# Every third feed-forward weight unit: the remainder by an accumulating on-chip transfer in place of a VectorE subtraction

## The chip, the core and the metric

The kernel runs on one core of one Trainium2 chip. The metric is the device time of one execution in microseconds (us). Before the change two timed runs took 1229.28 and 1230.01 us; their median is 1229.64 us.

## The reference

One layer of a decoder, on 256 tokens of width 2048, all in float32. The input is normalised and multiplied by one wide projection; three groups of heads (RWKV-7, gated DeltaNet, differential attention) work on the result; an output projection and a SwiGLU feed-forward follow, each added to the residual stream:

```
h = rms_norm(x, attn_norm_w)
p = h @ w_in
mixed = concatenate([rwkv7(p_rw), gated_deltanet(p_gdn), differential_attention(p_diff)])
x = x + mixed @ w_out
h = rms_norm(x, ffn_norm_w)
gate, up = split(h @ w_ffn_in)            # 2048 x 11264
x = x + (silu(gate) * up) @ w_ffn_out     # 5632 x 2048
```

The feed-forward reads w_ffn_in and w_ffn_out once, 138 MB of the 217 MB of all loads.

## The kernel before, in words

**Products in three parts.** A float32 number is held as a rounded part (`hi`, type float32r) and a remainder (`lo`). Activations and weights are both split so, and a product is the sum of three TensorE passes: hi by hi, lo of the weights by hi of the activations, hi of the weights by lo of the activations.

**Units.** The weights come as 410 units. A unit is two blocks of 128 rows by 512 columns: a tile of 128 partitions by 1024 float32, 512 KB. TensorE spends 12 matmuls of 512 columns on one: two halves of the tokens, two blocks, three passes, in the order hi, lo, hi for each block. Units 146 to 409 belong to the feed-forward: 176 of w_ffn_in and 88 of w_ffn_out.

**The weight stream.** `fetch_upto` (L218) issues the load of a unit into a buffer `raw` on SyncE's queue (L231). `stage_upto` (L234) splits a unit: ScalarE copies `raw` to `hi`, which rounds it (L245), and VectorE writes `lo` = `raw` - `hi` (L246). `take` (L250) is called when the products of unit u are written out, and stages unit u+3 (`LA` = 3). There are four buffers for `hi` and four for `lo`, so `hi` and `lo` of unit u+3 go where those of unit u-1 were, and can be written only when TensorE has read these for the last time. From unit 150 on (`plan["far"]` = 146 + `LA` + 1) loads run five units further ahead (`FAR` = 8), in nine buffers `raw`: the load of unit u+9 goes where unit u was, and waits until unit u has been split.

**Around it.** In the feed-forward ScalarE also has the SiLU (L121) and the rounding of the hidden columns (L1252), VectorE the products with the gate (L1267), the remainders of the hidden columns (L1253) and the residual sums (L1273). GpSimd's queue (POOL) holds only a few fills early in the program, and none in the feed-forward. What each engine runs, in which order, follows from the order of the calls and a scheduler that places the side work; each engine then runs its list in order, and an instruction waits on semaphores of the engines and transfers that it needs.

Of the kernel before, what the change touches and what calls it, by code (L numbers as in the profile page):

```python
# [8 lines left out]
F32 = mybir.dt.float32  # L9
F32R = mybir.dt.float32r  # L10
AF = mybir.ActivationFunctionType
ALU = mybir.AluOpType
# [81 lines left out]


class Acts:
    """Activation calls grouped by the table set that they need."""

    def __init__(self, tc):
        self.tc, self.nc = tc, tc.nc  # L100
# [27 lines left out]
def trunk(tc, A, out, dbg=None):  # L128
    nc = tc.nc
    V, S, G, TE = nc.vector, nc.scalar, nc.gpsimd, nc.tensor  # L130
# [38 lines left out]
        tog[0] ^= 1  # L169
        return rwbank() if tog[0] else gdbank()  # L170

    # ------------------------------------------------------------------ constants
    cst = pc.tile([P, CONST.shape[1]], F32, name="cst")
    vec = pc.tile([P, NV], F32, name="vec")

# [22 lines left out]
    rs1, lnr1, rsq64, ss2, rs2 = rst[:, 0:2], rst[:, 2:4], rst[:, 4:6], rst[:, 6:8], rst[:, 8:10]  # L198
    ssq = pc.tile([P, 8], F32, name="ssq")

    # ------------------------------------------------------------------ weight stream
    cm_raw, p_raw = pool("raw", 4)
    cm_hi, p_hi = pool("hi", 4)
    cm_lo, p_lo = pool("lo", 4)
# [2 lines left out]
    units = []  # L207
# [7 lines left out]
    state = {"fetched": 0, "next": 0}  # L215
# [19 lines left out]
    def stage_upto(i):  # L235
        fetch_upto(min(i + FIRST - LA, 2 * len(START) - 1))
        fetch_upto(i + FAR - LA if i >= plan["far"] else i)
        while state["next"] <= min(i, len(units) - 1):
            u = state["next"]
            srcs, nk, ns = units[u]  # L240
            n = sum(ns)
            hi = p_hi.tile([P, 1024], F32R, tag="hi", name=nm("hi"))
            lo = p_lo.tile([P, 1024], F32R, tag="lo", name=nm("lo"))
            r, h, l = raws.pop(u), hi[:, :nk * n], lo[:, :nk * n]
            S.copy(h, r)  # L245
            V.tensor_tensor(l, r, h.bitcast(F32), op=ALU.subtract)  # L246
            staged[u] = (h.rearrange("p (k c) -> p k c", c=n), l.rearrange("p (k c) -> p k c", c=n))
            state["next"] += 1

# [31 lines left out]
        plan["ffn"].append((h0, nh, ins_, outs_))  # L281
        h0 += nh

    # ------------------------------------------------------------------ side work, emitted between weight units
    jobs = []

    def spawn(gen, steps=0):
# [21 lines left out]
            advance(g)  # L309

    def after(first, then):
        """Keep the order of two instructions of one engine."""
        first, then = getattr(first, "ins", first), getattr(then, "ins", then)
        act._dep(then, first)

    def products(banks, ul, i, xs, n=512, parts=False):
        """What unit i of a chunk adds to its banks."""
        u, k0, nk = ul[i]
        wh, wl = take(u)
        if parts:  # L320
            seq = [(t, k, p_) for k in range(nk) for p_ in range(3) for t in range(2)]
        else:
            seq = [(t, k, p_) for t in range(2) for k in range(nk) for p_ in (0, 2, 1)]
        seen = [0, 0]
        for t, k, p_ in seq:
            seen[t] += 1
            xh, xl = xs(k0 + k)
            state["mm"] = TE.matmul(banks[t][:, 0:n], lhsT=(xl if p_ == 1 else xh)[:, t * P:(t + 1) * P],  # L328
                                    rhs=(wl if p_ == 2 else wh)[:, k, :], start=(i == 0 and seen[t] == 1),
                                    stop=(i == len(ul) - 1 and seen[t] == 3 * nk))  # L330

    def proj(ul, xs):
        """One chunk of 512 columns in token layout: two banks."""
        banks = [mmbank(), mmbank()]
        for i in range(len(ul)):
            products(banks, ul, i, xs)
            tick()
        return banks

    def rsq(out_, in_, scale=1.0, bias=None, b2=None):  # L340
        """out = (in*scale + bias)^-1/2 [* exp(b2)]"""
        act(out_, in_, AF.Ln, scale=scale, bias=eps_c[:in_.shape[0]] if bias is None else bias)
        if b2 is None:
            act(out_, out_, AF.Exp, scale=-0.5)
        else:
            act(out_, out_, AF.Exp, scale=-0.5, bias=b2)

    # ------------------------------------------------------------------ start: x and its norm
    cm_hT, p_hT = pool("hT")
    hTh = p_hT.tile([P, KT, T], F32R, name="hTh")  # L350
    hTl = p_hT.tile([P, KT, T], F32R, name="hTl")
# [6 lines left out]
    cm_x, p_x = pool("xp", side="right")  # L358
    x_in = A["x"].rearrange("(t p) d -> t p d", p=P)
    xT_in = A["xT"].rearrange("(k p) t -> p k t", p=P)  # L360
    # the array's clock rises while the first loads are on their way
    V.memset(xs1, 0.0)
    b = rwbank()
    for _ in range(WARM):
# [1 line left out]
    nc.scalar.dma_start(vec, A["vecs"])  # L366
    act.window(SET_NLE)
    def load_x():
        """x, transposed, in step with the units of the first chunks; then the constants."""
        xTs = {}  # L370

        def fetch_x(q):
            if q < len(START):
                k0, n = START[q]
                xTs[q] = p_x.tile([P, 2, T], F32, tag="xT", name=nm("xT"), bufs=FIRST // 2 + 1)
                (nc.sync if q else nc.scalar).dma_start(xTs[q][:, 0:n, :], xT_in[:, k0:k0 + n, :])
                fetch_upto(2 * q + 1)

        for q in range(FIRST // 2):
            fetch_x(q)  # L380
        for q, (k0, n) in enumerate(START):
            fetch_x(q + FIRST // 2)
            xT = xTs.pop(q)
            xsq = p_x.tile([P, 2, T], F32, tag="xsq", name=nm("xsq"), bufs=2)
            for j in range(n):
                k = k0 + j
                S.activation(hTh[:, k, :], xT[:, j, :], AF.Copy, scale=vcol("attn_w", k))
                V.scalar_tensor_tensor(hTl[:, k, :], xT[:, j, :], vcol("attn_w", k), hTh[:, k, :].bitcast(F32),
                                       op0=ALU.mult, op1=ALU.subtract)
            act(xsq[:, 0:n, :], xT[:, 0:n, :], AF.Square)  # L390
            for j in range(n):
                V.tensor_tensor(xs1, xs1, xsq[:, j, :], op=ALU.add)
            if q < 2:
                stage_upto(2 * q + 1)
            if q:
                yield
        nc.sync.dma_start(cst, A["const"])
        yield
        nc.sync.dma_start(lora[0:64, :], A["w_lora_b"])
        nc.sync.dma_start(lora[64:128, :], A["a_lora_b"])  # L400
        nc.sync.dma_start(glora, A["g_lora_b"])

    def first_norm():
# [7 lines left out]
        V.tensor_scalar(rsq64, rsq64, 1.0 / 64.0, None, op0=ALU.mult)  # L411
        V.tensor_scalar(lnr1, lnr1, -0.5, None, op0=ALU.mult)
        yield
        # small derived vectors
        V.tensor_scalar(omu, vcol("mu", 0, 14), -1.0, 1.0, op0=ALU.mult, op1=ALU.add)
        V.tensor_scalar(oka, vcol("k_a", 0, 4), -1.0, 1.0, op0=ALU.mult, op1=ALU.add)
        V.tensor_scalar(qw8, vcol("qn"), 0.125, None, op0=ALU.mult)
# [22 lines left out]
        products(banks_lora, plan["lora"], i, hx, 264, parts=True)  # L440
    close(cm_x)

    # ------------------------------------------------------------------ RWKV
    cm_tok, p_tok = pool("tok")
    cm_rq, prq = pool("rwq")
    sgx = prq.tile([P, T], F32, name="sgx")
# [38 lines left out]
    G.memset(XT[96:128, :, 0:32], 0.0)  # L485

    def tokens(banks, n=512):
        """Normalised rows of a chunk, one tile per 128 tokens."""
        res = []
        for t in range(2):  # L490
            tk = p_tok.tile([P, 512], F32, tag="tok", name=nm("tok"), bufs=TOKB)
            S.activation(tk[:, 0:n], banks[t][:, 0:n], AF.Copy, scale=rs1[:, t:t + 1])
            res.append(tk)
        return res

    def turned(toks, i, bank):
        """Column tiles 2i, 2i+1 of a chunk, columns on the partitions: bank[:, j*256 + t]."""
        for j in range(2):
            for t in range(2):
                TE.transpose(bank[:, j * T + t * P:j * T + (t + 1) * P],  # L500
                             toks[t][:, (2 * i + j) * P:(2 * i + j + 1) * P], ident)
        return bank
# [9 lines left out]

    KKRv = KKR.rearrange("p a c s t -> p (a c) s t")

    # inverse of the unit triangular blocks of 32, all at once, by forward substitution
    def forward_sub(n, fill, drain, Fa, Fx, Ft, per):
        scr = tc.dram_tile([n, 32, 32], F32, name=nm("scr"))
        scr2 = tc.dram_tile([n, 32, 32], F32, name=nm("scr2"))
# [142 lines left out]
    def rw_recur():  # L661
# [20 lines left out]
            return 2 * hp + par  # L682

        def read(c, which, rows):
            """Chunk c's tokens on the rows given: state times (r or kk), plus the part within the chunk."""
            b = rwbank()
            for hp in range(4):
                if c > 0:
                    TE.matmul(b[rows, hp * P:(hp + 1) * P], lhsT=KKR[:, hp, c, which, :], rhs=Sbd[:, hp, :],  # L689
                              start=(hp == 0), stop=False, skip_group_check=True)  # L690
            for h in range(8):
                TE.matmul(b[rows, h * 64:(h + 1) * 64], lhsT=AH[:, c, h % 2, h // 2, 64 * which:64 * which + 64],  # L692
                          rhs=VU[:, c, h, :], start=(c == 0 and h == 0), stop=True, skip_group_check=True)
            return b[rows, :]
# [56 lines left out]
    ready["rr"] = tokens(proj(plan["rr"], hx))  # L751
    ready["rv"] = tokens(proj(plan["rv"], hx))

    # ------------------------------------------------------------------ gated delta net
    banks_z = proj(plan["gz"], hx)
    while "rw_v" not in ready:
        tick()
# [281 lines left out]
            S.activation(mh, bv, AF.Copy, scale=vcol("gn"))  # L1039
            V.scalar_tensor_tensor(ml, bv, vcol("gn"), mh.bitcast(F32), op0=ALU.mult, op1=ALU.subtract)  # L1040

    # ------------------------------------------------------------------ differential attention
    def diff_evac(j, banks, res):
        qns = []
        for t in range(2):
# [138 lines left out]
            dj = spawn(diff_evac(j, banks, res), 1)  # L1184
        ready["d", g] = ops

    # ------------------------------------------------------------------ output projection
    def mixs(k):
        if k < 8:
            return mixh_a[:, k, :], mixl_a[:, k, :]  # L1190
# [46 lines left out]
    for cm in (cm_d, cm_mixrg, cm_rq, cm_tok):  # L1237
        close(cm)

    # ------------------------------------------------------------------ feed forward  # L1240
    cm_f, pf = pool("ffn")
    act.window(SET_SILU)
    out_v = out.rearrange("(t p) d -> t p d", p=P)
# [84 lines left out]
```

## Time and profile before

| | |
|---|---|
| timed runs | 1229.28 and 1230.01 us |
| profiled execution, first to last instruction (span) | 1227.3 us |
| timed median less this span | 2.3 us |
| TensorE busy | 1221.7 us, 100% of the span |
| VectorE busy | 710.2 us, 58% |
| ScalarE busy | 589.8 us, 48% |
| GpSimd busy | 5.8 us |
| mean granted clock of TensorE | 0.999 of full speed |
| data moved | 222.4 MB, 181 GB/s over the span |

The page is read from the chain that ended last: it says on which engine the end of the program hangs. Busy time of a matmul is modelled and overlaps with the next one (390 ns each, though a new one starts every 227 ns), so how close TensorE is to its limit is read from the starts of its matmuls, not from its busy share. The profiled execution has no time of its own beside the span; the 2.3 us between it and the median of the timed runs is taken for what lies around it.

### The profile page before, as it was taken

How to read it: one execution, taken by the hardware profiler on the slowest of the kernel's cores; microseconds unless marked ns; L12 is line 12 of the kernel's file. 1: busy time of each engine (PE TensorE's matmuls, PEld its weight loads, DVE VectorE, ACT ScalarE, POOL GpSimd, SP SyncE). 2: the span in 40 equal slices, each digit the busy share in tenths (PEclk: the TensorE clock that was granted, in tenths of full speed). 3: DMA queues.
4: the chain of work that ended last, by engine and by line, in shares of the span. 5: the costliest groups of instructions: out<-in, count | busy, mean ns of one | idle time of the engine just before them, and what ended most of it. 6: DMA issues, size and time to landing. Idle time of an engine off the chain costs nothing.

```text
span 1227.3 us, 15743 instructions
## 1 busy us (share of the span) xinstructions
PE 1221.7 (100%) x6062; PEld 1006.7 (82%) x6062; DVE 710.2 (58%) x972; ACT 589.8 (48%) x799; POOL 5.8 (0%) x11
## 2 busy tenths in 40 slices
PE   9999999999999999999999999999999999999998
PEld 8887888788888878888888888888888888888887
DVE  8585965699565766554454454544445445545553
ACT  7764454665446556544444444433344444444332
POOL 0100000000000000000000000000000000000000
PEclk9999999999999999999999999999999999999999
DMA  9755564256555545766666666566666666665660
GB/s 323 211 150 157 167 196 118 72 152 187 174 162 188 164 129 172 280 199 189 186 190 190 189 188 191 188 194 196 193 190 189 191 188 188 195 190 185 212 195 34
DMA packets 125082, 222.41 MB, mean 181 GB/s; under 512 B 15664, under 2 KB 19888, under 8 KB 125008
## 3 DMA queue, kind: packets, MB, share of 16 engines
q1 hardware_dynamic: 116848, 217.15, 58.6%
q10 hardware_dynamic: 8160, 4.27, 1.2%
q8 instruction: 47, 0.77, 0.2%
q14 instruction: 27, 0.22, 0.1%
HBM read 218.50 MB, written 2.88 MB: 180 GB/s over the span
## 4 chain that ended last, share of the span: by engine, by line
PE 99%; DMA 1%; ACT 0%; DVE 0%; issue 0%; SPq 0%
PE mm L328 90%; PE rw L500 1%; PE gd L500 1%; PE rw L692 1%; PE rw L622 1%; PE rw L1085 1%; PE rw L689 0%; PE rw L705 0%; DMA xT<-in_xT 0%; PE rw L562 0%; DMA vec<-in_vecs 0%; PE rw L1120 0%; PE gd L1120 0%; PE rw L676 0%; PE rw L668 0%; ACT s L121 0%
## 5 line engine op out<-in xcount | busy, mean ns | idle before, releaser
L246 DVE TENSOR_TENSOR lo<-raw,hi 128x1024 fp32r<-128x1024 f32 (+2 forms) x410 | 493.9, 1208 | 432.8 <-ACT hi L245 429.0
L245 ACT CAST hi<-raw 128x1024 fp32r<-128x1024 f32 (+2 forms) x410 | 425.2, 1039 | 535.3 <-PE mm L328 509.7
L328 PE MATMUL mm<-hi,hTh 128*128 128x512 f32 (+1 forms) x1152 | 448.9, 394 | 0.2
L328 PE MATMUL mm<-hi,hTl 128*128 128x512 f32 (+1 forms) x1152 | 441.4, 388 | 0.0
L328 PE MATMUL mm<-lo,hTh 128*128 128x512 f32 (+1 forms) x1152 | 441.1, 387 | 0.0
L328 PEld LDWEIGHTS mm<-hi,hTh 128*128 128x128 f32 x1152 | 215.6, 188 | 44.6 <-issue 1.1
L328 PEld LDWEIGHTS mm<-hi,hTl 128*128 128x128 f32 x1152 | 215.2, 188 | 45.1 <-issue 0.6
L328 PEld LDWEIGHTS mm<-lo,hTh 128*128 128x128 f32 x1152 | 215.4, 188 | 42.8 <-issue 1.1
L328 PE MATMUL mm<-hi,hidh 128*128 128x512 f32 x352 | 137.3, 390 | 0.0
L328 PE MATMUL mm<-hi,hidl 128*128 128x512 f32 x352 | 137.0, 389 | 0.0
L328 PE MATMUL mm<-lo,hidh 128*128 128x512 f32 x352 | 137.0, 389 | 0.0
L328 PEld LDWEIGHTS mm<-hi,hidl 128*128 128x128 f32 x352 | 66.1, 188 | 13.9
L328 PEld LDWEIGHTS mm<-hi,hidh 128*128 128x128 f32 x352 | 66.1, 188 | 13.6
L328 PEld LDWEIGHTS mm<-lo,hidh 128*128 128x128 f32 x352 | 66.1, 188 | 13.5
L328 PE MATMUL mm<-hi,mixh_a 128*128 128x512 f32 x64 | 26.0, 406 | 0.0
L328 PE MATMUL mm<-hi,mixh_d 128*128 128x512 f32 x64 | 25.9, 408 | 0.0
L328 PE MATMUL mm<-hi,mixl_d 128*128 128x512 f32 x64 | 25.4, 400 | 0.0
L328 PE MATMUL mm<-lo,mixh_d 128*128 128x512 f32 x64 | 25.4, 396 | 0.0
L328 PE MATMUL mm<-hi,mixl_a 128*128 128x512 f32 x64 | 25.3, 395 | 0.0
L328 PE MATMUL mm<-lo,mixh_a 128*128 128x512 f32 x64 | 25.2, 394 | 0.0
L121 ACT ACTIVATE sg<-mm,rst 128x512 f32<-128x512 f32 x22 | 15.2, 691 | 10.7 <-PE mm L328 10.7
L778 DVE SCALAR_TENSOR_TENSOR cacc<-gd,vec,cacc 128x255 f32<-128x255 f32 (+2 forms) x36 | 16.2, 477 | 5.8 <-ACT cacc L776 5.5
(301 smaller groups left out, 729.4 us busy)
## 6 DMA issues: line engine op xcount, KB each, us to landing
raw<-in_w_ffn_in SPq DMA_DIRECT2D x176, 512.0 KB, 3.8
raw<-in_w_in SPq DMA_DIRECT2D x103, 512.0 KB, 3.7
raw<-in_w_ffn_out SPq DMA_DIRECT2D x88, 512.0 KB, 4.5
raw<-in_w_out SPq DMA_DIRECT2D x32, 512.0 KB, 4.0
raw<-in_w_in SPq DMA_DIRECT2D x9, 256.0 KB, 5.7
xr<-in_x SPq DMA_DIRECT2D x8, 256.0 KB, 5.1
out<-xr ACTq DMA_DIRECT2D x8, 256.0 KB, 3.7
xT<-in_xT SPq DMA_DIRECT2D x7, 256.0 KB, 5.6
```

Of the source, the lines that this page charges most:

```text
L121: r = self.nc.scalar.activation(out, in_, func, **kw)
L245: S.copy(h, r)
L246: V.tensor_tensor(l, r, h.bitcast(F32), op=ALU.subtract)
L328: state["mm"] = TE.matmul(banks[t][:, 0:n], lhsT=(xl if p_ == 1 else xh)[:, t * P:(t + 1) * P], rhs=(wl if p_ == 2 else wh)[:, k, :], star ...
L500: TE.transpose(bank[:, j * T + t * P:j * T + (t + 1) * P], toks[t][:, (2 * i + j) * P:(2 * i + j + 1) * P], ident)
L622: TE.matmul(b[:, hp * P:(hp + 1) * P], lhsT=KB[rows, hp, c, :, :].rearrange("p s t -> p (s t)"), rhs=KKR[rows, hp, c, :, :].rearrange("p s ...
L692: TE.matmul(b[rows, h * 64:(h + 1) * 64], lhsT=AH[:, c, h % 2, h // 2, 64 * which:64 * which + 64], rhs=VU[:, c, h, :], start=(c == 0 and ...
L778: V.scalar_tensor_tensor(acc[:, sft:T], src[:, 0:T - sft], vcol("conv", 4 * ct + 3 - sft), acc[:, sft:T], op0=ALU.mult, op1=ALU.add)
L1085: TE.matmul(bk[m][:, hx_ * W:(hx_ + 1) * W], lhsT=qT[r, h, i * P:(i + 1) * P], rhs=kT_[r, h, 0:W], start=True, stop=True)
```

## The change

For units 150, 153, ..., 408 (87 of the 264 feed-forward units) VectorE no longer writes `lo`. ScalarE writes the negated, rounded weights into `lo`, and a transfer issued on GpSimd's queue then adds `raw` to `lo` in place, from on-chip memory to on-chip memory. The other units keep the subtraction. Comments that the diff also drops are left out here.

```diff
             S.copy(h, r)
-            V.tensor_tensor(l, r, h.bitcast(F32), op=ALU.subtract)
+            if u >= plan["far"] and u % 3 == 0:
+                S.activation(l, r, AF.Copy, scale=-1.0)
+                G.dma_start(l, r, accum_op=ALU.add)
+            else:
+                V.tensor_tensor(l, r, h.bitcast(F32), op=ALU.subtract)
             staged[u] = (h.rearrange("p (k c) -> p k c", c=n), l.rearrange("p (k c) -> p k c", c=n))
```

VectorE's list has 87 subtractions fewer (323 for 410), ScalarE's 87 instructions more, POOL's 87 transfers more. The lines behind the edit are four higher in the changed kernel (L332 is L328 before).

ScalarE, in the second half of the feed-forward (loads of w_ffn_out). The number in a name is a buffer's; `raw_6997` of before and `raw_7039` of the change hold the same unit. Before:

```order
L245 CAST hi_7035<-raw_6943 128x1024 [waits DMAHW5_49,DVE_49,PE_49]
L245 CAST hi_7053<-raw_6961 128x1024 [waits DMAHW6_49,DVE_49,PE_49]
L245 CAST hi_7071<-raw_6979 128x1024 [waits DMAHW7_49,DVE_49,PE_49]
L245 CAST hi_7089<-raw_6997 128x1024 [waits DMAHW0_49,DVE_49,PE_49]
L245 CAST hi_7107<-raw_7015 128x1024 [waits DMAHW1_49,DVE_49,PE_49]
L245 CAST hi_7129<-raw_7033 128x1024 [waits DMAHW2_49,DVE_49,PE_49]
L245 CAST hi_7147<-raw_7051 128x1024 [waits DMAHW3_49,DVE_49,PE_49]
```

The same place in the changed kernel:

```order
L247 ACTIVATE lo_7078<-raw_6984 128x1024 [waits DMASW6_49,DMAHW5_49,DVE_49,PE_49]
L245 CAST hi_7077<-raw_6984 128x1024 [waits PE_49,Activation_49]
L245 CAST hi_7096<-raw_7002 128x1024 [waits DMAHW6_49,PE_49,Activation_49]
L245 CAST hi_7114<-raw_7020 128x1024 [waits DMAHW7_49,DVE_49,PE_49]
L247 ACTIVATE lo_7133<-raw_7039 128x1024 [waits DMASW7_49,DMAHW0_49,DVE_49,PE_49]
L245 CAST hi_7132<-raw_7039 128x1024 [waits PE_49,Activation_49]
L245 CAST hi_7151<-raw_7057 128x1024 [waits DMAHW1_49,PE_49,Activation_49]
L245 CAST hi_7173<-raw_7075 128x1024 [waits DMAHW2_49,DVE_49,PE_49]
L247 ACTIVATE lo_7192<-raw_7094 128x1024 [waits DMASW0_49,DMAHW3_49,DVE_49,PE_49]
```

The negated copy of such a unit (L247) stands ahead of the rounding of the same unit (L245), not behind it.

SyncE's queue, at the loads that go where those units were (names with DMAHW are semaphores of loads, DMASW those of the transfers on POOL's queue). Before:

```order
L231 DMA raw_6979<-in_w_ffn_out 128x2x512 [waits DMAHW7_49,DVE_49]
L231 DMA raw_6997<-in_w_ffn_out 128x2x512 [waits DMAHW0_49,DVE_49]
L231 DMA raw_7015<-in_w_ffn_out 128x2x512 [waits DMAHW1_49,DVE_49]
L231 DMA raw_7033<-in_w_ffn_out 128x2x512 [waits DMAHW2_49,DVE_49]
L231 DMA raw_7051<-in_w_ffn_out 128x2x512 [waits DMAHW3_49,DVE_49]
```

The same loads in the changed kernel:

```order
L231 DMA raw_7020<-in_w_ffn_out 128x2x512 [waits DMAHW7_49,DVE_49]
L231 DMA raw_7039<-in_w_ffn_out 128x2x512 [waits DMAHW0_49,DMASW0_49,Activation_49]
L231 DMA raw_7057<-in_w_ffn_out 128x2x512 [waits DMAHW1_49,DVE_49]
L231 DMA raw_7075<-in_w_ffn_out 128x2x512 [waits DMAHW2_49,DVE_49]
L231 DMA raw_7094<-in_w_ffn_out 128x2x512 [waits DMAHW3_49,DMASW1_49,Activation_49]
```

Every third load now waits for the end of an accumulating transfer (DMASW), nine units back, and the two loads behind it in the queue wait with it.

TensorE, at the first matmuls of such a unit in the changed kernel:

```order
L332 MATMUL mm_7170<-hi_7114,hidl_4564 128x512
L332 MATMUL mm_7169<-hi_7132,hidh_4563 128x512 [waits Activation_49]
L332 MATMUL mm_7169<-lo_7133,hidh_4563 128x512 [waits DMASW3_49]
L332 MATMUL mm_7169<-hi_7132,hidl_4564 128x512
L332 MATMUL mm_7169<-hi_7132,hidh_4563 128x512
L332 MATMUL mm_7169<-lo_7133,hidh_4563 128x512
```

The second matmul of the unit waits for the transfer where it waited for VectorE; the order of the matmuls is that of before.

## Rows read from the trace of the kernel before

**Rows 1.** The page: span, busy engines, then the chain by line.

```profile
span 1227.3 us, 15743 instructions
PE 1221.7 (100%) x6062; PEld 1006.7 (82%) x6062; DVE 710.2 (58%) x972; ACT 589.8 (48%) x799; POOL 5.8 (0%) x11
...
PE mm L328 90%; PE rw L500 1%; PE gd L500 1%; PE rw L692 1%; PE rw L622 1%; PE rw L1085 1%; PE rw L689 0%; PE rw L705 0%; DMA xT<-in_xT 0%; PE rw L562 0%; DMA vec<-in_vecs 0%; PE rw L1120 0%; PE gd L1120 0%; PE rw L676 0%; PE rw L668 0%; ACT s L121 0%
```

**Rows 2.** Engines' busy time by stretch; behind POOL: clock, DMA share, GB/s.

```profile
550.00:1200.00 650.00, 650.00 (x2907) 538.10 (x2906) 321.19 (x289) 271.16 (x276) 0.00 (x0) 1.00 0.64 191
```

**Rows 3.** Timeline of TensorE over a change of unit; start, duration, engine, line.

```profile
799.07 0.39 PE L328 MATMUL mm<-lo,hidh 128*128 128x512 f32 x1
799.29 0.39 PE L328 MATMUL mm<-hi,hidl 128*128 128x512 f32 x1
799.52 0.39 PE L328 MATMUL mm<-hi,hidh 128*128 128x512 f32 x1
799.75 0.39 PE L328 MATMUL mm<-lo,hidh 128*128 128x512 f32 x1
...
807.91 0.39 PE L328 MATMUL mm<-lo,hidh 128*128 128x512 f32 x1
```

**Rows 4.** Timeline of ScalarE and VectorE there; brackets: idle before, and what ended it.

```profile
799.72 1.05 ACT L245 CAST hi<-raw 128x1024 fp32r<-128x1024 f32 x1 [1.67 <-PE mm L328]
800.81 1.22 DVE L246 TENSOR_TENSOR lo<-raw,hi 128x1024 fp32r<-128x1024 f32 x1 [1.49 <-ACT hi L245]
802.44 1.05 ACT L245 CAST hi<-raw 128x1024 fp32r<-128x1024 f32 x1 [1.67 <-PE mm L328]
```

**Rows 5.** Groups of instructions, 550 to 1200 us; busy, mean ns, idle before.

```profile
L246 DVE TENSOR_TENSOR lo<-raw,hi 128x1024 fp32r<-128x1024 f32 x235 | 288.0, 1225 | 327.5 <-ACT hi L245 324.4 <-DMA out<-xr 3.1
L245 ACT CAST hi<-raw 128x1024 fp32r<-128x1024 f32 x236 | 248.7, 1054 | 370.6 <-PE mm L328 370.6
```

**Rows 6.** Line 387 alone: a scaling copy on ScalarE, min, median, max ns.

```profile
L387 ACT ACTIVATE hTh<-xT,vec x16: 492/500/509, 5.3 to 28.8; 128x256 fp32r<-128x256 f32 x16
```

**Rows 7.** Transfers, 550 to 1200 us: the queue's share, then the loads' landing.

```profile
q1 hardware_dynamic: 63376, 122.17, 63.0%
...
DMA to landing us min/median/max: 3.5/3.9/5.9
```

**Rows 8.** Transfers, 500 to 517 us: rate, the queue's share, the loads' landing.

```profile
DMA packets 3422, 6.61 MB, mean 389 GB/s; under 512 B 205, under 2 KB 205, under 8 KB 3420
q1 hardware_dynamic: 3420, 6.59, 104.3%
...
DMA to landing us min/median/max: 5.1/10.0/10.9
```

**Rows 9.** Issues of loads on SyncE's queue, 550 to 1200 us, in ns.

```profile
L231 SPq DMA_DIRECT2D raw<-in_w_ffn_in x144: 367/368/368, 552.5 to 1080.2; - x144
```

**Rows 10.** Waits of SyncE's queue, 550 to 1200 us: total, times, longest.

```profile
SPq L231 <- DVE lo L246: 537.3, 232, 2.9
```

**Rows 11.** Groups of instructions on POOL, whole span.

```profile
L810 POOL MEMSET XG<- 128x1024 f32 x1 | 1.0, 957 | 156.8 <-DVE sm L848 156.8
```

## The prediction

> **What bounds the kernel now.** I read the chain that ended last first: it lies on TensorE almost from end to end, 90% of it in the unit products of L328 [rows 1]. Next the feed-forward by itself, where the whole change lies: from 550 to 1200 us TensorE is busy throughout at a granted clock of 1.00, while VectorE is busy 321 of 650 us, ScalarE 271, and the 16 transfer engines 0.64 of the time [rows 2]. The timeline shows matmul after matmul 0.23 us apart, across the border between two units too [rows 3]; a unit takes 2.72 us, the distance of two roundings [rows 4]. No gap is there that faster staging could close. The groups say the same: VectorE's subtraction sits idle for ScalarE's rounding, and the rounding for TensorE [rows 5]. Staging is driven by TensorE, which gives buffers back. So a gain has nowhere to come from. What is open is whether the longer way to `lo` still ends before TensorE needs it.
>
> **The slack of a unit before.** TensorE's last reading of a `lo` buffer starts at 799.07, of the `hi` buffer at 799.29 [rows 3]; the rounding into that `hi` starts at 799.72, 0.43 us after [rows 4]. The subtraction ends at 800.81 + 1.22 = 802.03. The unit is taken up three units later: its first `lo` matmul starts at 807.91 [rows 3], 799.75 plus three times 2.72. The present way has 5.9 us to spare.
>
> **What goes.** 87 subtractions of 1.225 us, 107 us of VectorE's time [rows 5]. They lie beside TensorE's work with 5.9 us to spare, so they are worth 0. Where VectorE's wait goes is of no matter, since nothing late hangs on it.
>
> **What comes on ScalarE.** 87 negated copies of 128x1024. The nearest rows are the rounding of the same shape, 1.05 us [rows 5], and a scaling copy of a quarter of it, 0.50 us [rows 6], whose four pieces would be 2.0; I take 1.05, since one instruction pays its start once. In a period of three units (8.16 us) ScalarE goes from 3.2 to 4.2 us for weights, and the rounding that is now behind the copy ends 1.05 us later, with over 6 us to spare. That costs 0; the cover is the three units of staging ahead.
>
> **The path of the transfer.** It starts when its `lo` buffer is free: 799.07 + 0.43 = 799.50 by the lag of the rounding. The copy ends at 800.55. TensorE needs the sum at 807.91. So from the end of the copy to landing the transfer has **7.36 us** at no cost. Call its real time D. If D is longer, TensorE stands still at the unit's second matmul, with all products behind it. Such a stop s puts off the need of the next accumulated unit, but not its start: its buffer is that of the unit before the stopped one, already read. So two stops in a row add up to D - 7.36, the mean stop is **(D - 7.36) / 2**, and 87 of them cost 43.5 us for each us of D above 7.36.
>
> **What D is.** No row shows a transfer on POOL's queue or an accumulation; I build D from the loads. With the transfer engines full, from 500 to 517 us, 389 GB/s pass [rows 8]: 512 KB (524 thousand bytes) take 1.35 us. The fastest landing of a load is 3.5 us [rows 7], so 2.15 us of it is not data. SyncE's issue is 0.37 us [rows 9]; for POOL's I take 0.96, its one instruction on a tile of this shape [rows 11], between the 0.37 of SyncE and, for two sources to describe, twice 0.96; it adds 0.6: 2.75 us beside the data. The data: an accumulation reads `raw` and also the `lo` that it adds to, so twice a load, 2.70 us. That makes 5.45 us alone. The bounds: below, one load's data and least landing, 3.5 us; above, a landing at full engines, 10.9 us [rows 8].
>
> The row for a load prices one source, and an addition that read its target for nothing would cost 1.35 and be hidden; a second source costs the stop. By the Trainium skill (Collectives: The Full Stack, Part 3, the bandwidth ceiling) an adding transfer runs at about half the rate of a copy, because of its two source reads and not of the addition; no run here shows that, and it would leave the sum as it is.
>
> **Sharing.** Loads come three to a period, 4.05 us of full engines, so with the transfer 6.75 of 8.16 us are taken: the engines can carry it. When they carry it matters. A load now waits for the landing of the transfer whose `raw` it overwrites, and two more queue behind it; before, SyncE waited for each subtraction apart, at most 2.9 us [rows 10]. So three loads bunch at each landing, and with D near 8 that is when the next transfer starts. If the two queues share the engines evenly, the 2.70 us become 5.40, and D = 2.75 + 5.40 = 8.15 us. I take this end rather than 5.45, as the bunching makes it. The held loads themselves are hidden: the slot is next read six units, 16.3 us, after the unit's own need, against a landing of at most 10.9.
>
> **The sum.** (8.15 - 7.36) / 2 = 0.40 us of stop, times 87: 34 us. Removed work 0, ScalarE 0, loads 0. 1227.3 + 34 = 1261.3 us of span, and 2.3 around it: **1264 us**, 2.8% over the median of 1229.64. The 2.3 is that median less the span of the one profiled execution.
>
> **Rivals.** (a) *The transfer is hidden.* At D up to 7.36 the time stays at about 1230; up to 7.93 it is less than 2% above (24.6 us are 0.283 us on each of 87). For it: 5.45 us if the loads don't collide, and also 5.45 if the accumulation costs the engines one load's data and does share. Against it: the bunching, and that every part of POOL's way is unmeasured. What decides is whether loads are in flight between copy and landing. By the Trainium skill (DMA: Bandwidth & Descriptors, Anatomy of one DMA) a transfer from GpSimd takes about 2.0 us and its bytes at 436 GB/s, an estimate of 3.2 us for one such tile; the trace's least load, 3.5 us, agrees, and by that rule even two sources shared evenly, some 6.8 us, stay hidden.
>
> (b) *The accumulation is slow in the transfer engines.* If it costs four loads' data instead of two, 5.40 us, a period needs 4.05 + 5.40 = 9.45 us of the engines, 1.29 us over 8.16, and 87 periods cost 112 us at least: 1342. By the path, 2.75 + 5.40 + 4.05 = 12.2 us give 2.42 us a stop, 210 us: 1440. It decides from an engine time above 4.1 us. For it: no row shows the rate of an addition. Against it: nothing in the trace asks for it.
>
> (c) *Faster by over 2%.* It would need 25 us from TensorE, which has no gaps in the feed-forward, at full clock. Only a shorter time between matmuls could give it, and the change does not touch them.
>
> **Chances.** Forecast (a stop of 0.28 to about 1.2 us, 1254 to 1335): 0.42. Hidden, or nearly: 0.40. Slow engines: 0.17. Faster: 0.01. So within 2% (about what a measurement of this kernel tells from no change) 0.40, slower 0.59. The range runs from 1228, just under no change, to 1345, where the slow case begins, which leaves out 0.18; the forecast's own range is 1254 to 1335.
>
> **What would show it.** The changed profile should show POOL's queue with 87 issues and a landing near 8 us; above 7.4 there must be idle time on TensorE before the `lo` matmul of every third feed-forward unit, released by that transfer, about 0.4 us each, and none before the other units. VectorE's busy time should fall by 107 us, ScalarE's rise by 91. SyncE's queue should wait on the transfer once in three loads, with three issues close together behind it. The share of the transfer engines should rise from 0.64 to about 0.8; well above that and near 1, rival (b) holds. The prediction is wrong if landing stays under 7 us, if TensorE waits for something else, such as a rounding or a load, or if the units before 150 change.

## The result, and the profile after

The changed kernel takes 1298.08 us (1296.03 to 1300.13, two runs) against 1229.64: 1.0556 times the time of before, with a 95% interval of 1.0516 to 1.0596. That is 68 us more. The forecast was slower, 1264 us, and the range 1228 to 1345 holds the result; of the loss, 34 us were forecast, half of what came.

The page of the changed kernel: span, busy engines, then the chain that ended last by engine and by line. It answers to [rows 1].

```profile
span 1298.3 us, 15999 instructions
PE 1242.3 (96%) x6062; PEld 1009.3 (78%) x6062; DVE 605.0 (47%) x885; ACT 670.9 (52%) x886; POOL 80.8 (6%) x98
...
issue 50%; PE 41%; POOL 5%; DMA 2%; ACT 1%; DVE 0%; POOLq 0%; SPq 0%; ACTq 0%
PE mm L332 34%; POOL lo L248 5%; DMA lo<-raw 1%; DMA raw<-in_w_ffn_in 1%; PE rw L696 1%; PE rw L626 1%; PE rw L1089 0%; PE rw L693 0%; PE rw L369 0%; PE rw L709 0%; PE rw L504 0%; PE rw L566 0%; POOLq L248 0%; ACT hi L245 0%; PE gd L504 0%
```

The span grew by 71.0 us. TensorE was not busy for 5.6 us of it before (1227.3 less 1221.7) and for 56.0 now: 50.4 us of the growth are standstill, 20.6 are busy time (longer matmuls, and at each stop the end of a matmul that no longer overlaps with the next). VectorE lost 105 us of work, and nothing came of that. The chain, which was TensorE's product line for 90%, now runs over POOL's transfer too; half of it is put to "issue", time for which the profile names no cause, so the reading below goes by TensorE's waits.

The waits of the changed kernel from 500 us on (engine and line, what was waited for, total us, times, longest), and the transfer's own rows (issue time in ns, then issue to landing):

```profile
PEld mm L332 <- DMA lo<-raw: 67.7, 42, 6.1
PE mm L332 <- DMA lo<-raw: 50.3, 36, 5.7
```

```profile
L248 POOL DMA_DIRECT2D lo<-raw x87: 859/859/1002, 502.6 to 1281.9; - x87
...
DMA to landing us min/median/max: 4.5/7.6/10.6
```

The 50.3 us of standstill all wait for the accumulating transfer, at 36 places of 87, 1.4 us each in the mean. And the landing is no one number: 4.5 to 10.6 us.

One such stop in the timeline, ScalarE, POOL and TensorE (brackets: idle before, and what ended it):

```profile
898.88 1.06 ACT L247 ACTIVATE lo<-raw 128x1024 fp32r<-128x1024 f32 x1 [1.44 <-PE mm L332]
```

```profile
900.24 0.86 POOL L248 DMA_DIRECT2D lo<-raw  x1 [7.30 <-ACT lo L247]
908.81 0.86 POOL L248 DMA_DIRECT2D lo<-raw  x1 [7.71 <-ACT lo L247]
```

```profile
907.26 0.39 PE L332 MATMUL mm<-hi,hidl 128*128 128x512 f32 x1
907.48 0.39 PE L332 MATMUL mm<-hi,hidh 128*128 128x512 f32 x1
909.81 0.50 PE L332 MATMUL mm<-lo,hidh 128*128 128x512 f32 x1 [1.94 <-DMA lo<-raw]
```

The negated copy ends at 899.94, POOL issues 0.3 us later, and TensorE goes on at 909.81, when the sum has landed 9.5 us after the issue. The next transfer is issued at 908.81, before that. It lands in 5.7 us and stops nobody.

SyncE's queue and the transfer queues (megabytes, share of 16 engines) from 550 to 1265 us, which answer to [rows 10] and [rows 7]:

```profile
SPq L231 <- DMA lo<-raw: 541.0, 79, 10.8
SPq L231 <- DVE lo L250: 39.0, 25, 3.2
```

```profile
q1 hardware_dynamic: 64431, 124.20, 53.7%
q0 software_dynamic: 11376, 41.42, 31.1%
```

SyncE waits for the landings, once for each transfer (78 are issued there), and hardly for VectorE any more. A transfer takes 0.311 x 715 / 78 = 2.85 us of all engines.

**What a landing depends on.** I took from the trace, for the 82 transfers between the first two and the last three, how many loads were issued just before the transfer, which here and below means from 2.0 us before its own issue to 0.3 us after it, and the mean landing:

| loads issued just before | transfers | mean landing, us |
|---|---|---|
| 0 | 16 | 5.9 |
| 1 | 32 | 7.0 |
| 2 | 11 | 9.1 |
| 3 | 23 | 8.7 |

At the very end, with no load in flight, it is 4.5 us. The loads that the transfer before has held come out when it lands; if the next one is issued within two microseconds after, it runs among them. The row of two is really one of three: all eleven have a third load between 2.4 us before and 0.8 us after their issue. Counted from 2.0 us before to 1.2 us after, none, one, two and three loads stand beside 7, 26, 8 and 41 transfers, which land in 5.9, 6.3, 7.6 and 8.7 us.

### The profile page after: what moved, and what is told of

It reads as the page before. It is cut to its first block, busy times and chain, and to the rows that moved or that the text cites. A ratio compares the mean times of both kernels' runs of the same rounds, so it can differ in the third digit from the quotient of the medians.

```text
span 1298.3 us, 15999 instructions
## 1 busy us (share of the span) xinstructions
PE 1242.3 (96%) x6062; PEld 1009.3 (78%) x6062; DVE 605.0 (47%) x885; ACT 670.9 (52%) x886; POOL 80.8 (6%) x98
## 4 chain that ended last, share of the span: by engine, by line
issue 50%; PE 41%; POOL 5%; DMA 2%; ACT 1%; DVE 0%; POOLq 0%; SPq 0%; ACTq 0%
PE mm L332 34%; POOL lo L248 5%; DMA lo<-raw 1%; DMA raw<-in_w_ffn_in 1%; PE rw L696 1%; PE rw L626 1%; PE rw L1089 0%; PE rw L693 0%; PE rw L369 0%; PE rw L709 0%; PE rw L504 0%; PE rw L566 0%; POOLq L248 0%; ACT hi L245 0%; PE gd L504 0%
## 5 line engine op out<-in xcount | busy, mean ns | idle before, releaser
L250 DVE TENSOR_TENSOR lo<-raw,hi 128x1024 fp32r<-128x1024 f32 (+1 forms) x323 | 387.0, 1203 | 574.0 <-ACT hi L245 568.5
L245 ACT CAST hi<-raw 128x1024 fp32r<-128x1024 f32 (+2 forms) x410 | 422.6, 1033 | 410.4 <-PE mm L332 249.9
L332 PE MATMUL mm<-lo,hTh 128*128 128x512 f32 (+1 forms) x1152 | 447.0, 393 | 35.7 <-DMA lo<-raw 35.6
L332 PE MATMUL mm<-hi,hTh 128*128 128x512 f32 (+1 forms) x1152 | 451.1, 396 | 0.0
L332 PE MATMUL mm<-hi,hTl 128*128 128x512 f32 (+1 forms) x1152 | 444.0, 390 | 0.0
L332 PEld LDWEIGHTS mm<-lo,hTh 128*128 128x128 f32 x1152 | 216.5, 189 | 90.6 <-DMA lo<-raw 47.9
L332 PEld LDWEIGHTS mm<-hi,hTh 128*128 128x128 f32 x1152 | 216.9, 189 | 45.4 <-issue 1.1
L332 PEld LDWEIGHTS mm<-hi,hTl 128*128 128x128 f32 x1152 | 216.8, 189 | 44.6 <-issue 0.6
L332 PE MATMUL mm<-lo,hidh 128*128 128x512 f32 x352 | 139.5, 396 | 14.8 <-DMA lo<-raw 14.7
L247 ACT ACTIVATE lo<-raw 128x1024 fp32r<-128x1024 f32 x87 | 92.2, 1060 | 117.0 <-PE mm L332 117.0
L332 PE MATMUL mm<-hi,hidh 128*128 128x512 f32 x352 | 138.4, 393 | 0.0
L332 PE MATMUL mm<-hi,hidl 128*128 128x512 f32 x352 | 138.2, 393 | 0.0
L248 POOL DMA_DIRECT2D lo<-raw x87 | 75.0, 862 | 977.8 <-ACT lo L247 691.0
L332 PEld LDWEIGHTS mm<-lo,hidh 128*128 128x128 f32 x352 | 66.7, 190 | 33.5 <-DMA lo<-raw 19.9
L332 PEld LDWEIGHTS mm<-hi,hidh 128*128 128x128 f32 x352 | 66.7, 189 | 14.1
L332 PEld LDWEIGHTS mm<-hi,hidl 128*128 128x128 f32 x352 | 66.7, 190 | 13.6
L332 PE MATMUL mm<-hi,mixh_a 128*128 128x512 f32 x64 | 26.0, 406 | 0.0
L332 PE MATMUL mm<-hi,mixh_d 128*128 128x512 f32 x64 | 25.9, 408 | 0.0
L332 PE MATMUL mm<-lo,mixh_d 128*128 128x512 f32 x64 | 25.4, 397 | 0.0
L332 PE MATMUL mm<-hi,mixl_d 128*128 128x512 f32 x64 | 25.4, 399 | 0.0
L332 PE MATMUL mm<-hi,mixl_a 128*128 128x512 f32 x64 | 25.3, 395 | 0.0
L332 PE MATMUL mm<-lo,mixh_a 128*128 128x512 f32 x64 | 25.2, 394 | 0.0
```

What stands on the lines that cost most here:

```text
L247: S.activation(l, r, AF.Copy, scale=-1.0)
L248: G.dma_start(l, r, accum_op=ALU.add)
```

## The experiments

Theory 1, *collision*: a transfer takes some 4.5 us alone and too long only when the held loads start just before it; the loss is lateness. Theory 2, *rate*: the adding transfer costs what it costs, by itself or because the transfer engines are near full. Each kernel is the changed one with the edit shown. Before ran beside each on the same chip, 1229.66 to 1229.93 us in the median.

**A ring of their own for the accumulated units' `raw`.**

```diff
-                raw = pf.tile([P, 1024], F32, tag="raw", name=nm("raw"), bufs=FAR + 1)
+                acc = u % 3 == 0
+                raw = pf.tile([P, 1024], F32, tag="rawa" if acc else "raw", name=nm("raw"), bufs=5 if acc else 6)
```

> The buffers raw of the accumulated units get a ring of their own (5), the others one of 6, so that no load waits for a transfer's landing and SyncE's loads no longer bunch behind it. Theory 1 (collision: a transfer takes some 4.5 us alone and 8 to 10 us only when three held loads start in the 1.5 us before it): landings narrow to 5.5 to 7.5 us, SyncE waits on VectorE again, few stops are left beyond the first one, 1231 to 1248 us. Theory 2 (rate: the adding transfer is slow by itself or the transfer engines are full, whatever the loads' order): landings stay near 7.5 us in the mean, 37 stops or more, 1285 to 1300 us.

1300.93 us, ratio 1.0601 (1.0569 to 1.0632): no better. It speaks for neither theory, because the edit did not do what it was to do. SyncE's waits from 550 to 1200 us:

```profile
SPq L232 <- DMA lo<-raw: 507.6, 73, 10.4
SPq L232 <- DVE lo L251: 33.1, 27, 2.9
```

The scheduler had moved each such load past four others up SyncE's list, to where it again waited for a landing, with the others behind it. A ring with more room does not loosen an in-order queue if the order may move with it.

**The transfer two units earlier.**

```diff
+            a = u + 2
+            if plan["far"] + 2 <= a < len(units) and a % 3 == 0:
+                early[a] = pf.tile([P, 1024], F32R, tag="loa", name=nm("lo"), bufs=2)
+                S.activation(early[a], raws[a], AF.Copy, scale=-1.0)
+                G.dma_start(early[a], raws[a], accum_op=ALU.add)
...
-            if u >= plan["far"] and u % 3 == 0:
-                S.activation(l, r, AF.Copy, scale=-1.0)
-                G.dma_start(l, r, accum_op=ALU.add)
-            else:
+            if u not in done:
```

> The negated copy and the transfer of an accumulated unit are issued two units earlier, into two buffers lo of their own; ring of raw and held loads as in the change (unit 150 keeps its subtraction). The slack grows from 7.36 to 12.8 us. Theory 1 (only lateness costs): every landing up to 10.9 us is in time, no stops, 1229 to 1234 us, although loads still bunch. Theory 2 (the transfer engines are the bound): earlier issue gives nothing lasting, 1280 us or more, transfer share near 1.

1230.61 us, ratio 1.0008 (0.9999 to 1.0018): all of the loss is gone. From 550 to 1200 us (busy by engine, clock, transfer share, GB/s), answering to [rows 2], and the transfer's landing over the whole run:

```profile
550.00:1200.00 650.00, 650.00 (x2907) 538.22 (x2906) 226.88 (x211) 344.51 (x355) 68.11 (x79) 1.00 0.92 255
```

```profile
DMA to landing us min/median/max: 4.5/5.1/9.8
```

The transfer engines are at 0.92, more than in the change (0.85), and TensorE does not stop there; its one stop for a transfer in the whole run is 0.6 us, at the first. So 264 loads and 86 additions pass in the time of before: theory 2 falls in its form of full engines. But the edit changed two things. The slack grew, and the landings shortened: 71 of 81 transfers now have no load issued just before them, and the loads are hardly held any more, against what was expected (SyncE waits 74.6 us for landings in this stretch). Through the rule used below, these landings would have cost some 5 us behind the first transfer at the old slack of 7.36 us too. So this run alone does not say how much of the loss was lateness and how much collision; the runs on the order of the loads, further down, keep the old slack.

**The transfer without the addition.** It copies `raw` to `lo`; the subtraction is left out.

```diff
-                G.dma_start(l, r, accum_op=ALU.add)
+                G.dma_start(l, r)
```

> The transfer copies raw to lo and adds nothing (the subtraction is left out, lo holds the whole weight); POOL's queue, sizes and waits stay. If the second source that an addition reads is what makes it long: the landing alone falls from 4.5 to about 3.5 us, the median from 7.6 to under 6, nearly all of the 37 stops go, 1230 to 1245 us. If POOL's way and the held loads make it long, whatever is added: landings and time stay within 15 us of the change, 1283 to 1300 us.

1248.29 us, ratio 1.0153 (1.0133 to 1.0173), 3 us above the upper end of the first answer and far from the second. From 550 to 1200 us:

```profile
L248 POOL DMA_DIRECT2D lo<-raw x77: 527/527/530, 554.1 to 1197.3; - x77
...
DMA to landing us min/median/max: 3.1/6.7/9.2
```

```profile
q0 software_dynamic: 10944, 39.85, 16.9%
```

A copy takes 0.169 x 650 / 77 = 1.43 us of all engines, an addition 2.85: twice. Its fastest landing in the whole run is 2.9 us against 4.5, its issue on POOL 0.53 us against 0.86. So the addition's price is real, and 50 of the 68 us hang on it; the remaining 19 us come even with a copy, so it is not the addition alone. The collisions stay: 42 of its 82 middle transfers have three loads just before them and land in 7.2 us in the mean.

**Every sixth unit.**

```diff
-            if u >= plan["far"] and u % 3 == 0:
+            if u >= plan["far"] and u % 6 == 0:
```

> Every sixth unit instead of every third: 44 transfers, 16.3 us apart. Theory 1 (collision with the loads that the transfer before has held): the next transfer starts some 8 us after a landing, finds one load in flight, lands in 5 to 6.5 us, no stop but the first, 1230 to 1240 us. Theory 2 (a price for each transfer): half of the loss, 1260 to 1267 us.

1237.47 us, ratio 1.0065 (1.0045 to 1.0085). Half of the transfers keep a ninth of the loss. The landings, and TensorE's only stop for a transfer (us, times):

```profile
  PE mm L332: 5.8, 1
...
DMA to landing us min/median/max: 4.5/5.4/8.9
```

One stop, the first; 38 of 39 middle transfers have one load just before them, and the 39 land in 5.4 us. A price for each transfer is excluded.

**The loads of two rings, kept in order.** As the first experiment, and each load is tied behind the one before it.

```diff
-                nc.sync.dma_start(r.rearrange("p (k c) -> p k c", c=n)[:, :, o:o + n_], src)
+                ld = nc.sync.dma_start(r.rearrange("p (k c) -> p k c", c=n)[:, :, o:o + n_], src)
+                if u > plan["far"]:
+                    after(state["ld"], ld)
+                state["ld"] = ld
```

> The two rings of the first experiment (6 and 5 buffers), and besides the loads of the feed-forward are kept in their order on SyncE's queue; in the first one they were moved up, to where they waited for a landing as before. By the places of the waits SyncE should now wait for VectorE alone, with two loads together about 1.5 us before each transfer and the third some 5 us later. Theory 1 (collision with the held loads): landings of 5.5 to 7.5 us, few stops beside the first, 1234 to 1255 us. Theory 2 (the order of the loads does not matter): 1285 to 1300 us as in the change and in the first experiment.

1277.32 us, ratio 1.0398 (1.0379 to 1.0416). Twenty-one of the 68 us are gone, less than theory 1 forecast and more than theory 2 allows. SyncE now waits for VectorE alone; the landings from 550 to 1200 us are still long:

```profile
SPq L232 <- DVE lo L254: 543.9, 149, 8.7
```

```profile
DMA to landing us min/median/max: 5.6/7.0/9.5
```

The holding is gone, but 81 of 82 middle transfers have two loads issued just before them (7.3 us in the mean), because the loads now wait for the staging and so come out in step with it. Theory 1 as first put, that the *held* loads do it, is too narrow: any loads just ahead do.

**One load ahead instead of two.** The same, and an accumulated unit's load stands behind that of the next unit.

```diff
             u = state["fetched"]
+            if u >= plan["far"]:
+                u += (1, -1, 0)[u % 3]
```

> As the kernel with two rings and kept order, but each accumulated unit's load stands behind that of the next unit. By the places of the waits one load starts some 1.5 us before each transfer and two start 4 us after its issue, where there two started before it and one after. Theory 1 (what counts is how many loads start just before a transfer: three in the change, 1298; two, 1277): landings fall to 5.5 to 6.7 us, no stops but the first (8 us), 1236 to 1248 us. Theory 2 (the mean load of the transfer engines counts, which is the same in all): about 1277 us.

1242.05 us, ratio 1.0095 (1.008 to 1.011), as theory 1 had it. Landings, and TensorE's stops in the whole run:

```profile
  PE mm L338: 9.3, 4
...
DMA to landing us min/median/max: 4.5/5.5/8.8
```

The same transfers, loads, rings and engines as in the kernel before it; only the place of one load in three on SyncE's queue differs. That is worth some 35 us. The transfer share from 550 to 1200 us rose from 0.88 to 0.90.

**A later start**, alone in the changed kernel, and together with the edit above.

```diff
-            if u >= plan["far"] and u % 3 == 0:
+            if u >= plan["far"] + 9 and u % 3 == 0:
```

> The first three accumulated units (150, 153, 156) keep their subtraction, 84 transfers are left. They fall into the stretch where nine loads of the feed-forward are filled in with the transfer engines full; the first transfer made TensorE stop for 5.7 us and the clock was at half for 6.8 us after it. If that stretch is a price of the start: 8 to 11 us less than the change, 1286 to 1291 us. If it only delays what any first transfer would cost: 1294 to 1299 us.

> The same, and the first three accumulated units keep their subtraction, as in the kernel with the later start. Theory 1: nothing of the loss is left, 1229 to 1234 us. If the first stop comes with any first transfer: 1236 us or more. Theory 2: 1270 us or more.

Alone: 1292.55 us, ratio 1.0514 (1.048 to 1.0548), between the two answers. That interval overlaps that of the change, and 42.3 us of standstill in 33 stops remain, so it tells little. Together with the order: 1232.05 us, ratio 1.0019 (1.001 to 1.0029), 10.0 us less than with the order alone; both keep the old slack. There the stretch at the start is a price of its own, and without it the first transfer stops nobody. In the changed kernel two things meet in that stretch: seven loads are in flight when the first transfer is issued at 502.6 us, which lands in 8.9 us, and its copy comes late, behind a rounding that waited for its load:

```profile
500.05 1.05 ACT L245 CAST hi<-raw 128x1024 fp32r<-128x1024 f32 x1 [1.81 <-DMA raw<-in_w_ffn_in]
501.00 1.05 ACT L247 ACTIVATE lo<-raw 128x1024 fp32r<-128x1024 f32 x1
```

The copy ends at 502.05; TensorE's last matmul before the stop starts at 505.51, so the sum was due at about 505.7. The slack was 3.7 us there, not 7.36, and even the least landing of 4.5 us would have been late.

**ScalarE's part alone.** The transfer is gone, VectorE subtracts in all units; the copies are overwritten.

```diff
-                G.dma_start(l, r, accum_op=ALU.add)
+                V.tensor_tensor(l, r, h.bitcast(F32), op=ALU.subtract)
```

> ScalarE's negated copies stay, the transfer is gone and VectorE subtracts in all units as before (the copies are then overwritten). If ScalarE's part costs nothing, as the prediction has it: 1229 to 1231 us. If the copies hold up the roundings behind them: 1235 us or more.

1229.65 us, ratio 0.9998 (0.9988 to 1.0008). The copies cost nothing.

By the number of loads issued just before a transfer, over the kernels in which it is nearly constant, and the change beside them:

| kernel | loads ahead | median landing of all, us | time, us |
|---|---|---|---|
| every sixth unit | 1 | 5.4 | 1237.47 |
| one load ahead | 1 | 5.5 | 1242.05 |
| one load ahead, later start | 1 | 5.5 | 1232.05 |
| two rings, kept order | 2 | 7.0 | 1277.32 |
| the change | 0 to 3 | 7.6 | 1298.08 |

None of the versions beats the kernel before. The best with a transfer, the early one, equals it with 94 us less work on VectorE from 550 to 1200 us (226.9 for 321.2), which TensorE has no use for.

## Why the prediction was right, and where it was short

**What bounds the kernel: right.** No version came under the time of before. VectorE's 107 us were worth 0, as priced; 105 went. ScalarE's copies cost 0, shown by the run with them alone. They took 1.06 us, priced at 1.05; ScalarE's busy time rose by 81 us where 91 were expected, because copy and rounding behind it overlap by 0.09 us.

**The path and its 7.36 us: right.** TensorE stops at the named matmul and at no other place that matters. Working the rule (a stop is D less 7.36 less the stop before, and never under 0) through the 86 measured D behind the first transfer gives 55.6 us of delay; the standstill of those transfers is 44.6 us on the matmuls' rows (50.3 less 5.7), plus about 0.16 us for each stop, since a matmul's 0.39 us overlap the next one's start. That is 50 us, and within 6 of the rule.

**D: near in its mean, wrong in its form.** From the end of the copy to landing it was 7.82 us in the mean, 8.15 were forecast. The parts: 0.3 us from the copy to POOL's issue and 0.86 of issue where 0.96 were taken; 4.8 us alone against 5.45; two sources, as taken, twice a copy's engine time by the run without addition. The Trainium skill's factor of about two for an adding transfer (Collectives: The Full Stack, Part 3, the bandwidth ceiling) is borne out by that run, 2.85 us to 1.43; that the second read makes it and not the addition, no run here separates. The held and bunched loads came as described. But I took the worst sharing as constant. It depends on how the next issue lies to the landing before it, and swings: a late landing stops TensorE, the next transfer is then already under way when the loads come out and is quick, the following ones come closer to the landings again, until one is in the midst of three loads.

**The sum: too small, and the step that fell short.** "The mean stop is (D - 7.36) / 2" holds only while every transfer is late. When D swings, a quick transfer gives nothing back to TensorE and still lets the next stop come in full. With the mean of 7.82 that formula gives 0.23 us on each of 87, 20 us; the same D one by one give 55.6. So the term of 34 us should have been about 50. Two more were missing. One is the first transfer, 5.7 us of standstill, for which the slack of 7.36 us was taken and 3.7 found. The other is the rest of the 20.6 us of busy time: 0.16 us at each of 36 stops, some 6 us, belong to the 50 and the first stop, and the other 15 come from the clock, below, and from the restart after a stop, where the first `lo` matmul takes 0.50 us for 0.39. The direction and the place of the stops were foreseen; that 1298 us lies in the range owes much to its width, up to 1345.

**The rivals.** (a), hidden, is what the early transfer shows, and what the order of the loads nearly reaches: its deciding point, whether loads are in flight between copy and landing, was the right one. The rule of the Trainium skill cited beside it (DMA: Bandwidth & Descriptors, Anatomy of one DMA) put even two sources with even sharing at an estimated 6.8 us; the trace has up to 10.6. (b), slow engines, is excluded: an addition takes 2.85 us of the engines, under the 4.1 from which it would decide, and 0.92 of the engines' time was reached without a stop. (c) did not come. The transfer share was foreseen at 0.8 and measured at 0.85.

What stays open: why loads that start just ahead of a transfer hold it up more than those that start just behind its issue; the 14 middle transfers issued over 0.3 us before the landing of the one before, with the held loads behind them, land in 5.8 us in the mean. The runs vary the order of the loads, not the way in which an engine picks between queues.

## What to carry to other kernels

A transfer put on the way to the bottleneck engine has to be judged by its slow landings against the slack, not by its mean, because early ones give nothing back: one by one, sum what each is late beyond the stop before it, and never under 0. If it holds a buffer that other transfers wait for, it lines them up behind its own landing, and the next one can run into them; look at the loads issued in the two microseconds before the issue of each transfer that lands late. Start it earlier, or move one load on the queue, before giving up on it, but ask first whether the engine that it relieves was needed.

## What the runs showed of the hardware that was not expected

TensorE's granted clock fell to half at some stops. Around the first one, in the changed kernel (busy by engine, then the clock, transfer share, GB/s), and the matmuls at its end:

```profile
509.20:515.90 6.70, 4.35 (x10) 3.46 (x11) 0.00 (x0) 0.00 (x0) 0.00 (x0) 0.50 1.04 293
```

```profile
511.55 0.79 PE L332 MATMUL mm<-lo,hTh 128*128 128x512 f32 x1 [5.66 <-DMA lo<-raw]
512.14 0.63 PE L332 MATMUL mm<-hi,hTl 128*128 128x512 f32 x1
512.57 0.63 PE L332 MATMUL mm<-hi,hTh 128*128 128x512 f32 x1
...
516.22 0.39 PE L332 MATMUL mm<-hi,hTh 128*128 128x512 f32 x1
516.45 0.39 PE L332 MATMUL mm<-lo,hTh 128*128 128x512 f32 x1
```

The clock was 0.50 of full speed, 1.2 of 2.4 GHz, while and after TensorE stood for 5.66 us, and the matmuls started 0.43 us apart instead of 0.23. The mean clock of the run is 0.992 of full speed against 0.999: 10.4 us of clock lost over 1298.3 against 1.2 before. There are four such stretches, at stops of 5.66, 2.21, 2.17 and 3.45 us, 20.5 us together, of which TensorE was busy for 16.5; stops of 2.31 and 2.14 us had none behind them. So some 8 of the 20.6 us of busy time are this: four of the 36 stops were paid for a second time.
